# GLA mixer and conv FFN on one core: output weights' gate products and block sums by GpSimd, SiLU and decays in a fixed order, FFN token loads ahead of norms, positions set anew

## The chip, the cores and the metric

The kernel runs on 1 core of one Trainium2 chip. Its time is the device time of one execution in microseconds. A core has TensorE (PE: matmuls; PEld: their weight loads), VectorE (DVE), ScalarE (ACT), GpSimd (POOL) and SyncE (SP, which issues most transfers here), each with an instruction queue that it works off in order, and engines for transfers between DRAM and the on-chip memories (SBUF, and PSUM, where matmuls accumulate).

## The reference

One layer of a decoder trunk: a gated linear attention (GLA) mixer, then a gated MLP with a causal convolution (conv FFN), each followed by a residual and a layer norm. There are 2048 tokens of 1024 features, in float32. Cut to what matters:

```python
def gla_mixer(h, w_in, w_a2, b_a, norm_g, w_o):        # 4 heads, dk 128, dv 256, chunks of 64 tokens
    q, k, v, r, a_lr = split(h @ w_in)
    log_a = log_sigmoid(a_lr @ w_a2 + b_a) / 16        # the decays
    bcum = cumsum(log_a, within a chunk)
    q_dec, k_inv, k_dec = q * exp(bcum), k * exp(-bcum), k * exp(blast - bcum)
    o = tril(q_dec @ k_inv.T) @ v + q_dec @ state      # state = state * exp(blast) + k_dec.T @ v
    o = o * rsqrt(mean(o * o) + eps) * norm_g
    return (o * silu(r)) @ w_o

def conv_ffn(h, w_up, conv_w, conv_b, w_down):
    u, g = split(h @ w_up)                             # 2 x 2816
    return (silu(causal_conv3(u) + conv_b) * g) @ w_down

def post_norm_residual(x, cs, w_mod, b_mod, ln_gain, ln_bias, sublayer):
    shift, scale, gate = split(cs @ w_mod + b_mod)     # cs = silu(c)
    y = sublayer(x * (1 + scale) + shift)
    return layer_norm(alpha * x + (1 + gate) * y, ln_gain, ln_bias)
```

The factor (1 + gate) of the mixer belongs to columns of w_o, so it can be multiplied into w_o before that product.

## The kernel before

**Products.** A float32 matrix is split into a high part (a cast on ScalarE, L104) and a low part (a subtraction on VectorE, L107), and each product of two tiles is three matmuls: high by high, high by low, low by high (mm3, L110 to L112). Large products are done in two-by-two blocks with seven block products in place of eight, in the order 0, 1, 5, 4, 6, 3, 2; the block sums that this needs of weights and tokens are done by `add` (L352), and accumulated results leave PSUM by `keep` (L446 to L448: a copy on ScalarE with a raised priority, names p and u). The bank that is copied is accumulated further by the next product, so that product waits for the copy.

**Stages, with their time in the trace.** Until about 60 us: modulated tokens, Q and K of the first block. Then, in units of TensorE's time that the tables of the program count: v_group(0) (units 0 to 14), r_group(0) (14 to 34, 4 iterations of r_iter), v_group(1) (34 to 48), r_group(1) (48 to 88, 8 iterations, about 320 to 497 us). An r_iter makes one 256-column block of the gate r or of q and k for two token blocks by seven products; with `prev` it finishes the iteration before: r_gate, r_up and r_end drain the banks, apply SiLU to r in halves and store it. From unit 88 (B0) follow the three segments of the last projections (SEG: Q of the second half, and the two output products OO0 and OO1) with the 16 (token block, head) pairs of the attention among them (head_l, head_r, ... head_n, head_d), the first layer norm (load_z, ln1, ln1_kt), until about 850; then the FFN up (to 1660) and down (to 2107).

**Decays.** For each of 16 (token block tb, head h) `decays` (L595 on) takes a tile A3 loaded from DRAM by a3_load (L590 to L592, two units earlier), makes one matmul (L607), and on ScalarE bias (L611), Abs (L612), Exp (L615), Ln (L620), on VectorE a minimum and a scan (L621, L622), then two Exp (L624, L625), and stores them (e_d, L626 and L627). SiLU and Exp/Ln are in different function tables of ScalarE; between them stands an ACT_TABLE_LOAD. `order(later, earlier)` pins an order of two instructions; last_silu and last_exp remember the last of each kind.

**Output weights.** w_fold(q, n) (L1105) loads one of 8 tiles of w_o (128x1024, name wo), multiplies it by 1 + gate (G, L1112) and stores it (wf_d); w_mix(q, n) (L1116) makes four block sums of each four tiles (L352) and stores them (wfc_d). The output products read both later. The gate's last piece is L297 (388 us).

**What sets the order.** `at_unit(u, f)` puts a step at a unit of TensorE's time; that gives the step's place and priority, and a scheduler then orders every engine's instructions by priorities and an estimate of when operands are ready. `tc.high_priority(offset)` raises a place. Only in the part from unit 88 is TensorE's order written out by hand. The tables (H_AT, STEP, XP_AT, D_AT, W..._AT, LN_AT, F_AT and so on) hold the units. All loads and stores are issued by SyncE (`load` and `store`), in order; a store that waits for its data holds up what stands behind it.

**FFN start.** first_w, part_end, x_first(0), x_first(1), first_w1, first_w2 (placed by F_AT) load the first weight tiles and token blocks of the FFN and make their block sums and splits; ln1 of the third token block (LN_AT[2]) falls in the same time, as do the last evictions of the output product (z).

Of the kernel before, what the change touches and what calls it, by code (L numbers as in the profile page):

```python
# [38 lines left out]
def kernel(  # L39
# [405 lines left out]
    def keep(po, name):  # L445
        t = t2p.tile([P, 512], F32, tag="t2", name=name)  # L446
        with tc.high_priority(offset=600):
            return t, nc.scalar.copy(t, po)  # L448
# [5 lines left out]
    if True:  # L454
# [9 lines left out]
        made = set()  # L464
        xrow = x.rearrange("(t p) d -> t p d", p=P)
# [123 lines left out]
        def a3_load(tb):  # L589
            assert ("a", tb) in made  # L590
            a3[tb] = t2p.tile([P, TB], F32R, tag="t2", name="A3")[0:96]
            load(a3[tb].bitcast(F32), a3_d[tb])  # L592

        def decays(tb, heads):
# [9 lines left out]
            A3 = a3.pop(tb)  # L604
            for h in heads:
# [20 lines left out]
                store(e_d[tb][h][:, lo], E1)  # L626
                store(e_d[tb][h][:, hi], E2)  # L627
# [80 lines left out]
        def qk_out(tb, h, pq, pk):  # L708
# [239 lines left out]
        def r_up(p, after=None):  # L948
# [4 lines left out]
            if p["W"]["kind"]:  # L953
                nc.scalar.copy(p["r0"][:, 512:1024], p["pa"])
                store(qk_d[tb][h], p["r0"])
# [5 lines left out]
            else:  # L961
                a = nc.scalar.activation(p["r0"][:, 512:1024], p["pa"], AF.Silu)
                nc.scalar.activation(p["r0"][:, 0:512], p["r0"][:, 0:512], AF.Silu)
                order(a, after)
            if last_exp:
                order(a, last_exp[-1])
            store(r_d[tb][h], p["r0"])

        def r_end(p, after=None):
# [9 lines left out]
            store(r_d[tb + 1][h], p["r1"])  # L979
# [124 lines left out]

        def w_fold(q, n):  # L1105
# [6 lines left out]
            nc.vector.tensor_tensor(rv, rv, g[:, None, :].to_broadcast([P, 2, 512]), op=ALU.mult)  # L1112
# [27 lines left out]
        R_AT = ((9.75, 10.25, 12.25), (42.75, 45.0, 45.25))  # L1140
# [3 lines left out]
        WAW_AT = (12.25, 45.75, 53.75)  # L1144
# [15 lines left out]
        M_AT = (36, 36.5, 37.75, 37.75, 40, 41, 41.75, 43.25, 51, 52, 53, 54, 55, 56, 57, 58)  # L1160
        MF_AT = (50.0, 49.5, 57.5, 62.5)
# [12 lines left out]
        WF_AT = ((69, 69.0, 70.0, 70.75), (72, 74.25, 75.5, 76.75))  # L1174
        WM_AT = ((72.0, 74.0), (82.75, 83.75))
# [5 lines left out]
        E_AT = (83.25, 85.45, 87.7, 88.45)  # L1181
# [114 lines left out]
        def head_t(H):  # L1296
# [4 lines left out]
            with tc.high_priority(offset=150):  # L1301
                nc.scalar.copy(H["KT"], pt)

        def head_a(H, g):
# [7 lines left out]
            with tc.high_priority(offset=1200):  # L1312
# [29 lines left out]
        def head_c(H, g):  # L1342
# [16 lines left out]
            with tc.high_priority(offset=600):  # L1359
# [11 lines left out]
        def head_d(H, e):  # L1371
# [4 lines left out]
            with tc.high_priority(offset=600):  # L1376
# [29 lines left out]
        def ln1_kt(tb, zs, kt, by_act=False):  # L1406
# [32 lines left out]
        def q_segment(tb):  # L1439
            key = "Q", tb  # L1440
            for ps_ in range(2):
                banks = [psum("mm", 4) for _ in range(4)]
                outs = [raw_tile("qk") for _ in range(2)]
                for u in range(4):

                    def done(n):
                        if u == 3:
# [137 lines left out]
        H_AT = (0.25, 1.5, 2.75, 4, 5, 6, 7, 8.25, 9.5, 12.75, 13.5, 14.75, 16.75, 18.5, 20, 21.5)  # L1585
        STEP = (-0.4, 0, 0.5, 0.6, 0.75, 0.2, 0.5, 0.85, 1, 1.5, 1.5, 1.6, 1.6, 2.3, 2.5)
        STEPB = (-0.5, 0, 0.5, 0.75, 1, 0.0, 0.25, 0.75, 1.0, 0.5, 1.75, 2, 2, 2.75, 3)
        for m in range(16):
            H = heads[m]
            u = B0 + H_AT[m]  # L1590
            for k, (f, *a) in zip(STEP if m < 8 else STEPB, ((head_l,), (head_s,), (head_t,), (head_a, 0), (head_a, 1), (head_v,), (head_i,), (head_b, 0),
# [3 lines left out]
                if f is head_r and m in (2, 14):  # L1595
                    k = 1.75
# [466 lines left out]
```

## Time and profile before

| what | value |
|---|---|
| runs | 2111.23, 2107.44, 2112.12 us (median 2111.23) |
| the profiled execution's own time | 2109.05 us |
| its span | 2107.0 us, granted clock 0.996 |
| TensorE busy | 2074.5 us (98%) |
| VectorE, ScalarE, GpSimd busy | 1532.0 (73%), 997.2 (47%), 109.8 us (5%) |
| SyncE's transfers | 568.16 MB, 76.6% of 16 engines' span |

A line of a group reads: line, engine, operation, output tile <- input tiles, shapes, count, then busy time in us, mean ns of one, and the idle time of the engine ahead of it with what ended it. A line of waits reads: what waited <- for what, us in total, times, longest. A line of the timeline reads: start, duration, engine, line, operation, and in brackets the idle time before it and its releaser. A line of windows gives the busy us and count of instructions of PE, PEld, DVE, ACT and POOL, then granted clock, DMA share and GB/s. A line of transfers has the median time from issue to landing at its end.

### The profile page before, as it was taken

To read this page: it belongs to the slowest core of one execution; us is meant where nothing else is said; L and a number is where in the kernel's file an instruction comes from. 1 tells how busy PE (TensorE), PEld (TensorE's weight loads), DVE (VectorE), ACT (ScalarE), POOL (GpSimd) and SP (SyncE) were. 2 spreads that over 40 slices of the span, in tenths; PEclk is the share of its full clock that TensorE was granted. 3 is DMA by queue.
4 is the path that set the end of the run, shared out by engine and by line. 5 is a ranking of instruction groups with operands and counts; after the bars stand their busy time and mean duration, and the time that the engine had idled before them with its cause. 6 is when DMAs were issued, how large, how long until landed. Compare 5 with 4: busy or idle time off the path is not lost.

```text
span 2107.0 us, 26146 instructions
## 1 busy us (share of the span) xinstructions
PE 2074.5 (98%) x9333; PEld 1713.0 (81%) x9333; DVE 1532.0 (73%) x2028; ACT 997.2 (47%) x1401; POOL 109.8 (5%) x254
## 2 busy tenths in 40 slices
PE   9999999999999999999999999999999999999998
PEld 7887887778888887888888888888888888888886
DVE  6855757776697868967787887666666797577557
ACT  4649735674554534644444453333333443354332
POOL 0000000001121301100000000000000000030001
PEclk9999999999999999999999999999999999999999
DMA  9787888689878897866796679777787897677662
GB/s 335 306 294 267 277 298 288 248 298 326 325 291 294 313 355 285 304 234 212 280 322 215 221 263 330 275 267 262 255 277 260 278 340 236 205 253 246 194 199 88
DMA packets 196210, 569.82 MB, mean 270 GB/s; under 512 B 25392, under 2 KB 36016, under 8 KB 186864
## 3 DMA queue, kind: packets, MB, share of 16 engines
q1 hardware_dynamic: 196080, 568.16, 76.6%
q8 instruction: 73, 1.20, 0.2%
q14 instruction: 57, 0.47, 0.1%
HBM read 366.49 MB, written 201.59 MB: 270 GB/s over the span
## 4 chain that ended last, share of the span: by engine, by line
PE 82%; DVE 6%; DMA 5%; ACT 4%; issue 2%; POOL 0%; SPq 0%; DVEq 0%; ACTq 0%; POOLq 0%
PE ps_mm L110 17%; PE ps_mm L112 17%; PE ps_mm L111 17%; PE ps_w L112 8%; PE ps_w L111 8%; PE ps_w L110 8%; PE ps_w L1354 1%; PE ps_w L1326 1%; PE ps_w L1356 1%; PE ps_w L1310 1%; DMA A<-a_d 1%; DMA mraw<-in_mws_dram 1%; PE ps_w L1412 1%; DVE hl L107 1%; PE ps_w L1375 1%
## 5 line engine op out<-in xcount | busy, mean ns | idle before, releaser
L110 PE MATMUL ps_mm<-xc,hl 128*128 128x512 f32 x920 | 362.6, 394 | 9.4 <-ACT u L448 7.7
L111 PE MATMUL ps_mm<-xc,hl 128*128 128x512 f32 x920 | 359.6, 391 | 0.0
L112 PE MATMUL ps_mm<-xc,hl 128*128 128x512 f32 x920 | 358.2, 391 | 0.0
L110 PEld LDWEIGHTS ps_mm<-xc,hl 128*128 128x128 f32 x920 | 173.5, 189 | 50.6 <-ACT u L448 10.9
L112 PEld LDWEIGHTS ps_mm<-xc,hl 128*128 128x128 f32 x920 | 173.6, 189 | 36.6 <-DVE hl L107 0.2
L111 PEld LDWEIGHTS ps_mm<-xc,hl 128*128 128x128 f32 x920 | 173.5, 189 | 35.9 <-issue 0.5
L112 PE MATMUL ps_w<-xc,hl 128*128 128x512 f32 x464 | 180.6, 389 | 2.0 <-DVE hl L107 2.0
L110 PE MATMUL ps_w<-xc,hl 128*128 128x512 f32 x464 | 180.8, 390 | 0.1
L111 PE MATMUL ps_w<-xc,hl 128*128 128x512 f32 x464 | 180.5, 389 | 0.0
L1660 DVE SCALAR_TENSOR_TENSOR ct<-U,cw_sb,ct 128x512 f32<-128x512 f32 x176 | 131.7, 748 | 23.8 <-ACT ct L1654 21.3
L104 ACT CAST hl<-wu 128x1024 fp32r<-128x1024 f32 x90 | 94.7, 1052 | 100.2 <-PE ps_mm L112 73.0
L448 ACT COPY u<-ps_mm 128x512 f32<-128x512 f32 x112 | 65.3, 583 | 161.9 <-PE ps_mm L112 153.4
L104 ACT CAST dhl<-raw 128x1024 fp32r<-128x1024 f32 x57 | 60.0, 1053 | 155.2 <-PE ps_mm L112 96.5
L107 DVE TENSOR_TENSOR hl<-wu,hl 128x1024 fp32r<-128x1024 f32 x90 | 109.9, 1221 | 28.0 <-ACT hl L104 27.5
L107 DVE TENSOR_TENSOR dhl<-raw,dhl 128x1024 fp32r<-128x1024 f32 x57 | 69.5, 1220 | 64.1 <-ACT dhl L104 64.0
L104 ACT CAST hl<-raw 128x1024 fp32r<-128x1024 f32 (+1 forms) x63 | 59.9, 954 | 106.7 <-PE ps_mm L112 42.0
L107 DVE TENSOR_TENSOR hl<-raw,hl 128x1024 fp32r<-128x1024 f32 (+1 forms) x63 | 69.1, 1102 | 53.0 <-ACT hl L104 52.9
L112 PEld LDWEIGHTS ps_w<-xc,hl 128*128 128x128 f32 x464 | 87.1, 188 | 20.5 <-DVE hl L107 2.4
L104 ACT CAST hl<-wg 128x1024 fp32r<-128x1024 f32 x56 | 58.9, 1052 | 94.6 <-PE ps_mm L112 85.5
L111 PE MATMUL ps_mm<-dhl 128*128 128x512 f32 x264 | 102.7, 389 | 0.0
L112 PE MATMUL ps_mm<-dhl 128*128 128x512 f32 x264 | 102.7, 389 | 0.0
L110 PE MATMUL ps_mm<-dhl 128*128 128x512 f32 x264 | 102.7, 389 | 0.0
(286 smaller groups left out, 4726.5 us busy)
## 6 DMA issues: line engine op xcount, KB each, us to landing
hc_d<-ct SPq DMA_DIRECT2D x154, 256.0 KB, 3.0
raw<-hc_d SPq DMA_DIRECT2D x70, 512.0 KB, 4.3
draw<-wc_d SPq DMA_DIRECT2D x70, 512.0 KB, 4.7
wu<-in_wup_dram SPq DMA_DIRECT2D x44, 512.0 KB, 5.1
wg<-in_wup_dram SPq DMA_DIRECT2D x44, 512.0 KB, 4.5
wh_d<-hl SPq DMA_DIRECT2D x22, 1024.0 KB, 4.8
hl<-wh_d SPq DMA_DIRECT2D x22, 1024.0 KB, 6.2
mraw<-in_mws_dram SPq DMA_DIRECT2D x40, 512.0 KB, 5.8
```

What stands on the lines that cost most here:

```text
L104: accs["copy"] = nc.scalar.copy(h, src)
L107: return nc.vector.tensor_tensor(l, src if lsrc is None else lsrc, h.bitcast(F32), op=ALU.subtract)
L110: nc.tensor.matmul(po, a[0], b[0], start=first, stop=False, skip_group_check=resumed)
L111: nc.tensor.matmul(po, a[0], b[1], start=False, stop=False, skip_group_check=resumed)
L112: return nc.tensor.matmul(po, a[1], b[0], start=False, stop=last, skip_group_check=resumed)
L448: return t, nc.scalar.copy(t, po)
L1310: nc.tensor.matmul(pav[:, i], KI[:, s * P:s * P + P], Q[:, s], start=True, stop=True)
L1326: nc.tensor.matmul(pst[:, s % 2 * DV:s % 2 * DV + DV], KTt[:, s * P:s * P + P], v[s], start=True, stop=True)
L1354: nc.tensor.matmul(pos_, at[:, i], v[s], start=True, stop=st is None)
L1356: nc.tensor.matmul(pos_, Q[:, s, 0:128], st, start=False, stop=True)
L1375: nc.tensor.transpose(pt[:, s * P:s * P + P], on[:, s, e * P:e * P + P], ident)
L1660: nc.vector.scalar_tensor_tensor(ct, U[:, o + i:o + i + 512], cw_sb[:, j, i:i + 1], ct, op0=ALU.mult, op1=ALU.add)
```

## The change

- c and the modulation biases (c_sb, mbs_sb) are loaded from ScalarE's queue at the start, in place of SyncE's.
- `keep` has a priority offset of 1200 in place of 600. In the attention part the offsets of four operations change: the K transposes' copy 150 to 60, the attention masks 1200 to 300, the copy of o 600 to 0, the gating of o 600 to 1200; that of the first head's loads goes from 1200 to 60.
- r_up: the second half's SiLU is pinned behind the last exponentials and the first half's behind it; r_up's SiLU now counts as the last one (last_silu), so that later decays' exponentials are pinned behind it.
- a3_load's tile is kept per (token block, heads), not per token block. There are 16 loads as before.
- The products of w_fold and the sums of w_mix are GpSimd's (W_ENG).
- Nearly all tables of units change, a little each. st_e to st_m are names for `store` (ACT_ST is empty), and D_BY is 1: these change nothing.

On ScalarE, the rows between two copies u of r_group(0), in the stretch 183 to 193 us of the profile; r, mn and az are tiles of the gate and of decays. Before:

```order
L104 CAST hl<-wu 128x1024
L624 ACT_TABLE_LOAD
L624 ACTIVATE mn<-az 128x512
L611 ACTIVATE mn<-ps_w,ba_sb 128x512
L625 ACTIVATE az<-az 128x512
L962 ACT_TABLE_LOAD
L962 ACTIVATE r_1526<-ps_mm 128x512
L612 ACTIVATE az<-mn 128x512
L104 CAST h_1832<-s_1672 128x512
L615 ACT_TABLE_LOAD
L615 ACTIVATE az<-az 128x512
L448 COPY u_1826<-ps_mm 128x512
```

The same stretch of the change (from here on its lines are 2 to 10 further):

```order
L448 COPY u_1734<-ps_mm 128x512
L626 ACTIVATE mn<-az 128x512
L104 CAST hl<-wu 128x1024
L627 ACTIVATE az<-az 128x512
L964 ACT_TABLE_LOAD
L964 ACTIVATE r_1554<-ps_mm 128x512
L968 ACTIVATE r_1554<-r_1554 128x512
L448 COPY u_1812<-ps_mm 128x512
```

Two of three table loads left the stretch, the next decays' first operations stand behind the copy, and both halves of the SiLU share one load. Over the program the order has 34 ACT_TABLE_LOAD rows before and 25 now.

On SyncE, at the first four tiles of w_o in r_group(1), about 399 to 417 us. wf_d are the folded tiles, wfc_d their sums, A the decays' loads (A_3439 and A_3457 are for the ninth and tenth decays, in this order). Before:

```order
L1113 DMA wf_d_252<-wo 128x1024
L967 DMA r_d_2_342<-r_3164 128x1024
L1113 DMA wf_d_254<-wo 128x1024
L979 DMA r_d_2_346<-r_3242 128x1024
L592 DMA A_3439<-a_d_266 96x512
L940 DMA wu<-in_wab_dram 128x1024
L1125 DMA wfc_d_0_258<-wo 128x1024
L941 DMA wg<-in_wab_dram 128x1024
L1125 DMA wfc_d_0_262<-wo 128x1024
```

The change:

```order
L1122 DMA wf_d_250<-wo 128x1024
L594 DMA A_3382<-a_d_266 96x512
L974 DMA r_d_2_342<-r_3161 128x1024
L943 DMA wg<-in_wab_dram 128x1024
L1122 DMA wf_d_252<-wo 128x1024
L1122 DMA wf_d_254<-wo 128x1024
L986 DMA r_d_2_346<-r_3258 128x1024
L942 DMA wu<-in_wab_dram 128x1024
L1134 DMA wfc_d_0_258<-wo 128x1024
L1134 DMA wfc_d_0_262<-wo 128x1024
L943 DMA wg<-in_wab_dram 128x1024
L594 DMA A_3457<-a_d_266 96x512
```

The tenth decays' load (A_3457) now stands behind the stores of two sums, which wait for GpSimd; the ninth's stands behind two folded tiles. GpSimd's own order has the 16 operations as four folds, four sums, four folds, four sums, ahead of the attention's small operations.

On VectorE, at the FFN start (about 825 to 840 us; z are evictions of the output product, xs and xc the FFN's token block, hl<-wg and hl<-wu splits of its first weights). Before:

```order
L352 TENSOR_TENSOR z<-z,ps_mm 128x512 x3
L107 TENSOR_TENSOR hl<-wu,hl 128x1024
L352 TENSOR_TENSOR xs<-xs 128x1024
L352 TENSOR_TENSOR z<-z,ps_mm 128x512
L352 TENSOR_TENSOR xs<-xs,xc 128x1024
L107 TENSOR_TENSOR hl<-wg,hl 128x1024
L352 TENSOR_TENSOR xs<-xs 128x1024
L107 TENSOR_TENSOR xc<-xc 128x1024
L352 TENSOR_TENSOR xs<-xc,xs 128x1024
L107 TENSOR_TENSOR xc<-xs,xc 128x1024
L107 TENSOR_TENSOR xc<-xc 128x1024
L107 TENSOR_TENSOR xc<-xs,xc 128x1024
```

The change:

```order
L352 TENSOR_TENSOR xs<-xs,xc 128x1024
L352 TENSOR_TENSOR z<-z,ps_mm 128x512
L352 TENSOR_TENSOR xs<-xs 128x1024
L107 TENSOR_TENSOR xc<-xc 128x1024
L352 TENSOR_TENSOR xs<-xc,xs 128x1024
L107 TENSOR_TENSOR xc<-xs,xc 128x1024
L107 TENSOR_TENSOR xc<-xc 128x1024
L107 TENSOR_TENSOR xc<-xs,xc 128x1024
L352 TENSOR_TENSOR z<-z,ps_mm 128x512
L107 TENSOR_TENSOR hl<-wg,hl 128x1024
```

Six operations of the token block moved ahead of hl<-wg. TensorE's order moved with them: of the product with hl<-wg, the first matmul with the low part stood at row 3164 of TensorE's order and stands now at row 3187.

The diff, cut to its core (of the tables, the rows that the text speaks of):

```diff
-    load(c_sb, cT)
+    nc.scalar.dma_start(c_sb, cT)
...
-    load(mbs_sb, mbs)
+    nc.scalar.dma_start(mbs_sb, mbs)
...
     def keep(po, name):
         t = t2p.tile([P, 512], F32, tag="t2", name=name)
-        with tc.high_priority(offset=600):
+        with tc.high_priority(offset=1200):
             return t, nc.scalar.copy(t, po)
...
         def at_decays(u, tb, heads):
-            at_unit(u - 2, a3_load, tb)
+            at_unit(u - 2, a3_load, tb, heads)
...
-        def a3_load(tb):
+        def a3_load(tb, heads):
             assert ("a", tb) in made
-            a3[tb] = t2p.tile([P, TB], F32R, tag="t2", name="A3")[0:96]
-            load(a3[tb].bitcast(F32), a3_d[tb])
+            a3[tb, heads] = t2p.tile([P, TB], F32R, tag="t2", name="A3")[0:96]
+            load(a3[tb, heads].bitcast(F32), a3_d[tb])
...
             else:
                 a = nc.scalar.activation(p["r0"][:, 512:1024], p["pa"], AF.Silu)
-                nc.scalar.activation(p["r0"][:, 0:512], p["r0"][:, 0:512], AF.Silu)
                 order(a, after)
+                if last_exp:
+                    order(a, last_exp[-1])
+                a2 = nc.scalar.activation(p["r0"][:, 0:512], p["r0"][:, 0:512], AF.Silu)
+                order(a2, a)
+                a = a2
             if last_exp:
                 order(a, last_exp[-1])
-            store(r_d[tb][h], p["r0"])
+            last_silu.append(a)
+            st_r(r_d[tb][h], p["r0"])
...
+        W_ENG = (nc.vector, nc.gpsimd)[1]
...
-            nc.vector.tensor_tensor(rv, rv, g[:, None, :].to_broadcast([P, 2, 512]), op=ALU.mult)
+            W_ENG.tensor_tensor(rv, rv, g[:, None, :].to_broadcast([P, 2, 512]), op=ALU.mult)
...
-                add(nc.vector, r22, r21, r22)
-                add(nc.vector, r21, r11, r21, SUB)
+                add(W_ENG, r22, r21, r22)
+                add(W_ENG, r21, r11, r21, SUB)
                 return
-            add(nc.vector, r11, r22, r11, SUB)
-            add(nc.vector, r12, r12, r11, SUB)
+            add(W_ENG, r11, r22, r11, SUB)
+            add(W_ENG, r12, r12, r11, SUB)
...
-        D_AT = (17, 20, 22.75, 26.75, 50.5, 54, 58, 62, 70, 72, 74, 76, 78, 80, 82, 84)
+        D_AT = (17, 20, 23.0, 26.75, 50.5, 54, 58, 60, 68, 70, 72, 76, 78, 80, 82, 84)
...
-        XP_AT = (16.5, 19.75)
+        XP_AT = (14.5, 21.75)
...
-        WF_AT = ((69, 69.0, 70.0, 70.75), (72, 74.25, 75.5, 76.75))
-        WM_AT = ((72.0, 74.0), (82.75, 83.75))
+        WF_AT = ((69, 69.0, 70.5, 71.25), (73.75, 75.5, 76.25, 77.5))
+        WM_AT = ((72.0, 74.5), (84.25, 84.5))
...
-            with tc.high_priority(offset=600):
+            with tc.high_priority(offset=0):
                 nc.scalar.copy(on[:, 2 * g:2 * g + 2].rearrange("p s c -> p (s c)"), po)
...
-            with tc.high_priority(offset=600):
+            with tc.high_priority(offset=1200):
                 nc.vector.scalar_tensor_tensor(sr[:, e], pt, ng_sb[:, e:e + 1], sr[:, e], op0=ALU.mult, op1=ALU.mult)
...
-        H_AT = (0.25, 1.5, 2.75, 4, 5, 6, 7, 8.25, 9.5, 12.75, 13.5, 14.75, 16.75, 18.5, 20, 21.5)
+        H_AT = (0.75, 1.5, 2.75, 4, 5, 6, 7, 8.25, 9.5, 12.75, 13.5, 14.75, 16.75, 18.5, 20, 21.5)
...
-        LN_AT = ((17, 18.25, 17.5, 18.0), (21, 21.25, 21.5, 21.75), (32.5, 32.75, 33, 33.25))
+        LN_AT = ((17, 18.25, 17.5, 18.0), (21, 21.25, 21.5, 21.75), (34.25, 34.5, 34.75, 35))
...
-        F_AT = (28, 29.5, 34, 32, 34.5)
+        F_AT = (28, 29.5, 32.5, 32, 34)
```

More of the change, by code (lines that the diff above doesn't have):

```diff
@@ L464 @@
         made = set()
+        ACT_ST = ''
+        st_e, st_q, st_x, st_r, st_n, st_m = [nc.scalar.dma_start if c in ACT_ST else nc.gpsimd.dma_start if c.upper() in ACT_ST else store for c in "eqxrnm"]
         xrow = x.rearrange("(t p) d -> t p d", p=P)
@@ L603, in decays @@
             assert ("a", tb) in made
-            A3 = a3.pop(tb)
+            A3 = a3.pop((tb, heads))
             for h in heads:
@@ L625, in decays @@
                 last_exp.append(nc.scalar.activation(E2, az, AF.Exp, scale=-1.0 / 16.0))
-                store(e_d[tb][h][:, lo], E1)
-                store(e_d[tb][h][:, hi], E2)
+                st_e(e_d[tb][h][:, lo], E1)
+                st_e(e_d[tb][h][:, hi], E2)
                 made.add(("E", tb, h))
@@ L644, in keep_a @@
             nc.scalar.copy(t, pa[0:96])
-            store(ak_d[hf], t)
+            st_e(ak_d[hf], t)
             made.add(("ak", hf))
@@ L978, in r_end @@
             last_silu.append(a)
-            store(r_d[tb + 1][h], p["r1"])
+            st_r(r_d[tb + 1][h], p["r1"])
         staged = []
@@ L1143 @@
                 at_unit(V0 + u, f, *a)
-        WAW_AT = (12.25, 45.75, 53.75)
+        WAW_AT = (12.75, 45.75, 53.75)
         for u in WAW_AT:
@@ L1148 @@
         at_unit(GR_AT[0], gate_rows, 1, X)
-        D_AT = (17, 20, 22.75, 26.75, 50.5, 54, 58, 62, 70, 72, 74, 76, 78, 80, 82, 84)
-        for m, u in enumerate(D_AT):
-            at_decays(u, m // 4, (m % 4,))
-        XP_AT = (16.5, 19.75)
+        D_AT = (17, 20, 23.0, 26.75, 50.5, 54, 58, 60, 68, 70, 72, 76, 78, 80, 82, 84)
+        D_BY = 1
+        for m in range(0, 16, D_BY):
+            at_decays(D_AT[m], m // 4, tuple(range(m % 4, m % 4 + D_BY)))
+        XP_AT = (14.5, 21.75)
         for pr in range(2):
@@ L1237, in open_act @@
             pools["act"] = actx.enter_context(tc.tile_pool(name="actp", bufs=1, reuse_waits="tile"))
-            with tc.high_priority(offset=1200):
+            with tc.high_priority(offset=60):
                 head_l(heads[0])
@@ L1300, in head_t @@
             H["KT"] = t2p.tile([P, TB], F32, tag="t2", name="KTt")
-            with tc.high_priority(offset=150):
+            with tc.high_priority(offset=60):
                 nc.scalar.copy(H["KT"], pt)
@@ L1311, in head_a @@
             am = attm[H["h"] % 2 * 2 + g]
-            with tc.high_priority(offset=1200):
+            with tc.high_priority(offset=300):
                 nc.vector.copy_predicated(am[0:64], mask[0:64, None, :].to_broadcast([64, 2, P]), pav[0:64, :, 0:128])
@@ L1396, in ln1 @@
             normalise(zs[t], after)
-            store(zn_d[tb * 4 + t], zs[t])
+            st_n(zn_d[tb * 4 + t], zs[t])
         cols = {}
@@ L1595 @@
                 if f is head_r and m in (2, 14):
-                    k = 1.75
+                    k = -1.25
                 at_unit(u + k, f, H, *a)
         SEG = (("Q", 1), ("OO", 0), ("OO", 1))
-        XO_AT = (7, 8.75, 10.75, 12.75, 14.75, 15.5, 18.0)
+        XO_AT = (7, 8.75, 10.75, 12.75, 14.5, 13.5, 18.0)
         for u, i in zip(XO_AT, OP):
             at_unit(B0 + u, o_x, i)
-        YX_AT = (19.75, 21.75)
-        YS_AT = (23.0, 23.0)
+        YX_AT = (19.5, 22.5)
+        YS_AT = (24.5, 24.5)
         for n in range(2):
```

34 lines of the change are left out of this document (17 added, 17 removed).

## The prediction

> **What bounds the kernel now.** I read the page first, then what TensorE waited for, then the stretches where it lost time.
>
> ```profile
> span 2107.0 us, 26146 instructions
> PE 2074.5 (98%) x9333; PEld 1713.0 (81%) x9333; DVE 1532.0 (73%) x2028; ACT 997.2 (47%) x1401; POOL 109.8 (5%) x254
> PE ps_mm L110 <- ACT u L448: 10.2, 9, 3.2
> PE ps_w L1375 <- ACT on L1369: 2.3, 3, 1.0
> PE ps_w L112 <- DVE hl L107: 2.0, 1, 2.0
> PE ps_w L607 <- DMA A<-a_d: 1.9, 2, 1.5
> PE ps_mm L112 <- DVE xg L107: 1.5, 1, 1.5
> ```
>
> TensorE is idle for 2107.0 − 2074.5 = 32.5 us, and the change touches no product. So all it can win is a part of those 32.5 us, plus the slow matmuls that follow a stall. The longest wait is for ScalarE's copy of a PSUM bank (u, by keep), which frees the bank for the next product. The stretches show where the other engines are short (PE, PEld, DVE, ACT, POOL busy, then clock, DMA):
>
> ```profile
> 175.00:200.00 25.00, 23.21 (x94) 18.46 (x93) 15.52 (x20) 24.66 (x30) 0.00 (x0) 0.93 0.77 268
> 200.00:225.00 25.00, 25.00 (x111) 20.68 (x111) 15.46 (x17) 24.45 (x31) 0.00 (x0) 1.00 0.58 199
> 425.00:450.00 25.00, 24.39 (x105) 19.24 (x104) 20.22 (x23) 19.85 (x30) 0.00 (x0) 1.00 0.88 311
> 825.00:850.00 25.00, 21.67 (x89) 16.08 (x88) 23.55 (x27) 16.11 (x21) 0.20 (x2) 1.00 0.69 243
> 1000.00:1025.00 25.00, 25.00 (x120) 20.85 (x120) 18.31 (x26) 11.00 (x17) 0.38 (x3) 1.00 0.77 263
> ```
>
> ScalarE is full in 175–225 (24.66 and 24.45 of 25), VectorE in 825–850 (23.55). Later the FFN runs without a gap (1000–1025), so it has nothing to give.
>
> **SiLU and decays in a fixed order.** A table load stands before each change of function on ScalarE:
>
> ```profile
> L597 ACT ACT_TABLE_LOAD x7 | 9.0, 1283 | 0.1
> L624 ACT ACTIVATE mn<-az 128x512 f32<-128x512 f32 x16 | 10.1, 632 | 7.2 <-DVE az L622 7.0
> 183.57 0.57 ACT L448 COPY u<-ps_mm 128x512 f32<-128x512 f32 x1
> 184.04 1.05 ACT L104 CAST hl<-wu 128x1024 fp32r<-128x1024 f32 x1
> 185.11 1.28 ACT L624 ACT_TABLE_LOAD   x1
> 191.08 1.28 ACT L615 ACT_TABLE_LOAD   x1
> 192.91 0.57 ACT L448 COPY u<-ps_mm 128x512 f32<-128x512 f32 x1
> 193.53 0.58 PE L110 MATMUL ps_mm<-xc,hl 128*128 128x512 f32 x1 [1.79 <-ACT u L448]
> 197.28 0.40 PE L110 MATMUL ps_mm<-xc,hl 128*128 128x512 f32 x1
> ```
>
> The rows on order count 34 loads before and 25 after, so 9 × 1.283 = 11.5 us of ScalarE go. At 183–193 the work between two copies was 192.91 − 184.04 = 8.9 us with three loads. In the changed order it is one load (1.28), one weight cast (1.05), two exponentials and two half SiLUs at 0.63: 4.8 us. The second copy could then run at 184.0 + 4.8 = 188.8, and TensorE arrives at 193.53 − 1.79 = 191.7. The new order adds no wait between engines: the SiLUs stand behind the copy and the exponentials of their own engine, and behind them a copy (after one product more) and casts that had 1.28 us loads there before. The wait goes. So do the slow matmuls: nine took 197.28 − 193.53 = 3.75 us, where the rate of 200–225 (111 in 25.00, 0.225 each) asks for 2.0. Together **−3.5 us**; I see no case that makes it less than −1.8.
>
> The longest stall and the next decays:
>
> ```profile
> 169.89 0.80 PE L110 MATMUL ps_mm<-xc,hl 128*128 128x512 f32 x1 [3.16 <-ACT u L448]
> 343.17 0.47 PE L607 MATMUL ps_w<-A,w2s 96*128 96x512 f32 x1 [1.51 <-DMA A<-a_d]
> ```
>
> Up to 165 us ScalarE's and SyncE's orders are the same in both kernels but for one SiLU, whatever XP_AT says; ScalarE is held there by the token prepared through DRAM (x_prep). 169.89 stays: 0. The remaining 10.2 − 3.2 − 1.8 = 5.2 us of waits for u are spread over seven places of both r_groups. Fewer table loads, and a copy with more priority (keep, 600 to 1200), work there: **−2** (bounds 0 and −5). At 343.17 the load of A was queued behind two stores of decays and now stands ahead of them: **−1.5** (0 to −1.9).
>
> **Gate products and sums on GpSimd.** Sixteen operations leave VectorE:
>
> ```profile
> L352 DVE TENSOR_TENSOR wo<-wo 128x1024 f32<-128x1024 f32 x8 | 9.8, 1219 | 1.1 <-DMA wf_d<-wo 1.0
> L1112 DVE TENSOR_TENSOR wo<-wo,G 128x1024 f32<-128x1024 f32 x8 | 9.7, 1221 | 4.0 <-DMA wo<-in_wab_dram 4.0
> L1253 POOL MEMSET attm<- 128x256 f32 x4 | 1.1, 312 | 0.0
> L190 POOL MEMSET maskf<- 128x128 f32 x1 | 0.2, 204 | 0.0
> ```
>
> That frees 19.5 us of VectorE, which in 425–450, its fullest stretch there, has 4.8 of 25 us free anyway: worth nothing on the path by itself. GpSimd's price isn't in the trace. Its memsets grow by 108 ns for 128 columns, so 1024 columns of one stream cost at least 0.2 + 0.84 × 0.9 = 1.0 us, and three streams (two read, one written) 2.7. I take t = 2.3, nearer the upper end, since two operands share what one memset has alone. The Trainium skill (GPSIMD Engine Reference, Elementwise) gives 4497 ns for 2048 columns, an estimate of 2.25 here; the sum would be the same by it.
>
> What is late next is on SyncE's queue, which is in order: the stores of these tiles wait for GpSimd, and loads of A stand behind them. The rows:
>
> ```profile
> 388.35 0.68 DVE L297 SCALAR_TENSOR_TENSOR G<-ps_w,graw 128x512 f32<-128x512 f32 x1
> wf_d<-wo SPq DMA_DIRECT2D x8, 512.0 KB, 3.4
> A<-a_d SPq DMA_DIRECT2D x8, 192.0 KB, 4.1
> 414.57 0.40 PE L607 MATMUL ps_w<-A,w2s 96*128 96x512 f32 x1
> ```
>
> On the old clock, the gate is ready at 389.0, and the first fold begins about 389.5. Four folds end at 389.5 + 4t. The sums overwrite tiles that are being stored, so they wait for the landing (3.4, say 5 with the queue). Two sums, 2t, release the two stores ahead of the load for the tenth decays, whose issue and landing take 0.4 + 4.1. Counted in the orders, the ninth decays' product was the 1582nd matmul of 512 columns and ran at 414.57; now the tenth's is the 1583rd, so TensorE needs this load at 414.8 on that clock. The stall is 389.5 + 6t + 9.5 − 414.8 = 6t − 15.8: nothing at t = 2.3, 0.4 at 2.7, 5 at 3.5. The loads ahead and behind have more room. I put **+2** for this and for VectorE's share (bounds 0 and +10).
>
> **Attention.** Heads, output loads and the three priorities move, mostly by exchanging neighbours on VectorE; the distance from the norm (L1369) to its transposes (L1375) stays, so its 2.3 us stay. The 1.5 us for xg may go, since xg now stands between evictions instead of behind seven: **−1** (bounds −5 and +3: all waits of this part, or as many new ones as xg and the norm cost now).
>
> **FFN start.**
>
> ```profile
> 832.55 0.50 PE L112 MATMUL ps_w<-xc,hl 128*128 128x512 f32 x1 [2.00 <-DVE hl L107]
> 823.11 0.69 DVE L352 TENSOR_TENSOR z<-z,ps_mm 128x512 f32<-128x512 f32 x1 [0.64 <-PE ps_mm L112]
> 827.26 1.23 DVE L107 TENSOR_TENSOR hl<-wu,hl 128x1024 fp32r<-128x1024 f32 x1 [0.74 <-ACT hl L104]
> 828.40 1.22 DVE L352 TENSOR_TENSOR xs<-xs 128x1024 f32<-128x1024 f32 x1
> 831.27 1.22 DVE L107 TENSOR_TENSOR hl<-wg,hl 128x1024 fp32r<-128x1024 f32 x1
> 844.02 1.21 DVE L107 TENSOR_TENSOR hl<-wu,hl 128x1024 fp32r<-128x1024 f32 x1
> ```
>
> Before, VectorE idled 0.64 to 0.74 four times at evictions and a split (823–827), 2.7 us in all, and did most of the token block behind hl<-wg. In the new order six operations of that block, 1.14 apart (827.26 to 828.40), come ahead of hl<-wg and fill that idle time: this split ends near 832.4 + 6.8 − 2.7 = 836.5. But TensorE's order moved too and asks for its low half 23 matmuls later: 832.55 − 2.00 + 23 × 0.225 = 835.7. The next split (844.02) comes some 3.5 us earlier, with those six done. I count 1 us of stall where 825–850 lost 25.00 − 21.67 = 3.3, and a little won just around it: **−3** (bounds −4.5 and +2, if the later hl<-wg is waited for after all).
>
> c and its table from ScalarE's queue move only the first 3 us: 0 (±1).
>
> **Sum.** −3.5 − 2 − 1.5 + 2 − 1 − 3 = −9 us. The profiled execution took 2109.05, the three runs 2107.44 to 2112.12 with a median of 2111.23; the four average 2110. That gives **2101 us**. A measurement here tells 0.2% (4.2 us) from no change.
>
> **Rivals.**
>
> *No change, 2108.* Only 193.53 is won and the waits for u move to the next thing late, as at 169.89: 2110 − 3.5 + 2 = 2108.5. For it: seven of the nine waits for u are short (5.2 us in all) and stand among casts which stay. Against: three different stretches improve in the order.
>
> *Slower, 2117.* GpSimd and VectorE exclude each other, and the tenth decays' load comes late. The trace shows that GpSimd can be held:
>
> ```profile
> 1038.95 1.22 DVE L107 TENSOR_TENSOR hl<-wu,hl 128x1024 fp32r<-128x1024 f32 x1
> 1039.07 1.15 POOL L1731 COPY halo<-U 128x2 f32<-128x2 f32 x1 [16.19 <-DVE U L352]
> L1731 POOL COPY halo<-U x22: 184/185/2245, 866.3 to 1274.6; 128x2 f32<-128x2 f32 x22
> ```
>
> A copy of 185 ns took 1.15 us and ended with the split beside it. One such wait per operation gives t = 2.3 + 1.2 = 3.5, a stall of 5. Without GpSimd's term the sum is −11; so 6t − 15.8 = 11, t = 4.5, is the point from which nothing is left, and t = 5.5 gives 2110 − 11 + 17 = 2116, and 2117 with a little for VectorE, held in return. It needs two to three waits in each operation, so VectorE would have to cut into one that is running; against it stands that VectorE is idle 19% of its fullest stretch there.
>
> *Held in turn, 2107.* Each operation of GpSimd waits once for VectorE and then holds it to its own end. From the rows above, that is t = 3.5 and a stall of 5, and VectorE is held for up to 16 × 2.3 = 37 us where 19.5 were freed, 17 more in a stretch of about 80 us with some 20 us idle; I put 3 us for splits that come late by it: 2110 − 11 + 5 + 3 = 2107. For it: the copy that ended with the split. Against: VectorE's own durations stay at 1.22 beside GpSimd in that row, though for a copy too short to show it. This is what the Trainium skill says (SBUF — State Buffer, the shared port pair): whichever of GpSimd and a VectorE operation with two SBUF inputs starts first has the port to its end.
>
> *More, 2093.* The attention's and all of u's waits shrink too, or 169.89 goes with its slow matmuls (5 us): 2110 − 9 − 8. Little speaks for the latter, as ScalarE's order there is unchanged.
>
> **How the numbers follow.** Forecast 0.51, more 0.12, no change 0.11, held in turn 0.12, slower 0.14. Held in turn lies at the edge of 0.2%: a sixth of it counts as faster. Faster: 0.51 + 0.12 + 0.02 = 0.65; same 0.11 + 0.10 = 0.21; slower 0.14. The range 2090 to 2113 takes the gain to −20 on the one side; on the other it takes in the no-change case and a stall up to t = 4.9, and leaves out the worst of the slower one. The forecast's own range is 2096 to 2106.
>
> **What would show it.** Right: 25 table loads, no wait at 193, 169.89 still there, no wait for A near 343, folds of 2–3 us on GpSimd, and at 825–850 more than 23 us of TensorE. Wrong: folds over 4 us, a wait of L607's successor for A around 400–415 of several us, or new waits for attention's tiles after 500.

## The result and the profile after

The changed kernel takes 2121.08 us (median of six runs, 2118.03 to 2130.59). The kernel before takes 2112.16 us (2107.44 to 2113.91, six runs). The ratio is 1.0053, with a 95% interval of 1.0037 to 1.0070: slower by about 11 us. The forecast was 2101, and its range ended at 2113. The profiled execution took 2120.55 us with a span of 2118.8, so the two profiles that are compared below differ by 2118.8 − 2107.0 = +11.8 in their spans.

The head of the page and the waits of TensorE in the changed kernel:

```profile
span 2118.8 us, 26149 instructions
PE 2077.1 (98%) x9333; PEld 1715.0 (81%) x9333; DVE 1536.9 (73%) x2012; ACT 984.7 (46%) x1392; POOL 155.2 (7%) x270
PE ps_w L609 <- DMA A<-a_d: 8.9, 2, 4.6
PE ps_mm L110 <- ACT u L448: 7.5, 6, 4.3
PE ps_w L112 <- DVE hl L107: 5.9, 1, 5.9
```

The copies u cost less than before (7.5 against 10.2), and ScalarE is busy 12.5 us less (984.7 against 997.2), as its nine table loads fewer should make it. But two loads of A and one split of VectorE now cost 14.8 us, where waits of those two kinds cost 3.9. VectorE is the line to stop at: it has 16 operations fewer, worth 19.5 us, and is busy 4.9 us *more*. The stretches from 375 to 475 (PE, PEld, DVE, ACT, POOL, clock, DMA). Before, the first two of them:

```profile
375.00:400.00 25.00, 24.14 (x106) 18.93 (x105) 18.00 (x26) 19.46 (x25) 0.00 (x0) 1.00 0.61 218
400.00:425.00 25.00, 24.65 (x109) 20.05 (x109) 19.42 (x22) 15.67 (x21) 0.00 (x0) 1.00 0.87 318
```

The change, all four:

```profile
375.00:400.00 25.00, 18.29 (x77) 14.23 (x78) 17.58 (x18) 17.43 (x23) 11.57 (x4) 0.94 0.48 167
400.00:425.00 25.00, 20.64 (x83) 16.56 (x82) 18.21 (x13) 10.16 (x14) 10.61 (x4) 0.91 0.62 211
425.00:450.00 25.00, 25.00 (x104) 20.16 (x105) 11.57 (x15) 22.29 (x32) 9.73 (x4) 0.94 0.82 317
450.00:475.00 25.00, 20.01 (x79) 15.80 (x78) 21.13 (x18) 13.73 (x22) 11.07 (x4) 0.87 0.67 239
```

TensorE did 343 matmuls in these 100 us. GpSimd has four operations in each stretch. VectorE did 18 operations in 17.58 us and 13 in 18.21 us, where it had done 26 in 18.00 and 22 in 19.42 before: it is as busy with far fewer. In the third stretch, though, TensorE waits for nothing beside GpSimd's four operations: it is busy for all of the 25.00 us. The timeline of VectorE and GpSimd in the first stretch shows why:

```profile
384.51 11.57 POOL L1121 TENSOR_TENSOR wo<-wo,G 128x1024 f32<-128x1024 f32 x4 [382.78 <-DVE G L297]
385.48 2.84 DVE L624 TENSOR_TENSOR_SCAN az<-smask,mn 128x512 f32<-128x512 f32 x1
388.82 0.68 DVE L352 TENSOR_TENSOR r<-ps_mm,p 128x512 f32<-128x512 f32 x1
389.53 1.54 DVE L352 TENSOR_TENSOR s<-wu,wg 128x512 f32<-128x512 f32 x1
391.11 2.76 DVE L352 TENSOR_TENSOR wg<-wg 128x512 f32<-128x512 f32 x1
393.91 2.71 DVE L352 TENSOR_TENSOR wu<-wg,wu 128x512 f32<-128x512 f32 x1
396.54 0.68 DVE L107 TENSOR_TENSOR h<-s,h 128x512 fp32r<-128x512 f32 x1
397.75 1.21 DVE L107 TENSOR_TENSOR hl<-wg,hl 128x1024 fp32r<-128x1024 f32 x1
399.01 0.80 PE L112 MATMUL ps_w<-xc,hl 128*128 128x512 f32 x1 [5.86 <-DVE hl L107]
```

The four folds run from 384.51 to 396.08. In that time wg and wu, operations of 128x512 with both operands in SBUF, take 2.76 and 2.71 us, about the length of a fold (2.39 undisturbed), and after 396.08 the same kind takes 0.68. The scan at 385.48, also with both operands in SBUF, takes 2.84 where it takes 1.22 undisturbed; s, which comes in the last third of a fold, takes 1.54. The one with an operand in PSUM (r<-ps_mm,p at 388.82) takes 0.68 in the middle of it. So block sums and splits queue up behind GpSimd, TensorE waits 5.86 us for the split hl, and then runs 11 matmuls in 4.87 us (399.01 to 403.88, where 2.5 would do).

### The profile page after: what moved, and what is told of

Its sections match the earlier page's. It is cut to its first block, busy times and chain, and to the rows that moved or that the text cites. A ratio compares the mean times of both kernels' runs of the same rounds, so it can differ in the third digit from the quotient of the medians.

```text
span 2118.8 us, 26149 instructions
## 1 busy us (share of the span) xinstructions
PE 2077.1 (98%) x9333; PEld 1715.0 (81%) x9333; DVE 1536.9 (73%) x2012; ACT 984.7 (46%) x1392; POOL 155.2 (7%) x270
## 4 chain that ended last, share of the span: by engine, by line
PE 82%; DMA 7%; DVE 5%; ACT 3%; issue 2%; POOL 1%; SPq 0%; DVEq 0%; ACTq 0%; POOLq 0%
PE ps_mm L110 17%; PE ps_mm L112 17%; PE ps_mm L111 17%; PE ps_w L112 8%; PE ps_w L110 8%; PE ps_w L111 8%; PE ps_w L1336 1%; PE ps_w L1364 1%; DMA mraw<-in_mws_dram 1%; PE ps_w L1366 1%; PE ps_w L1320 1%; DMA graw<-in_mwg_dram 1%; DVE hl L107 1%; PE ps_w L1422 1%; DVE xc L107 0%
## 5 line engine op out<-in xcount | busy, mean ns | idle before, releaser
L112 PE MATMUL ps_w<-xc,hl 128*128 128x512 f32 x464 | 182.9, 394 | 5.9 <-DVE hl L107 5.9
L110 PE MATMUL ps_w<-xc,hl 128*128 128x512 f32 x464 | 182.6, 394 | 0.0
L111 PE MATMUL ps_w<-xc,hl 128*128 128x512 f32 x464 | 182.5, 393 | 0.0
L112 PEld LDWEIGHTS ps_w<-xc,hl 128*128 128x128 f32 x464 | 88.3, 190 | 25.1 <-DVE hl L107 6.5
L110 PEld LDWEIGHTS ps_w<-xc,hl 128*128 128x128 f32 x464 | 88.5, 191 | 18.7 <-ACT hl L104 0.4
L111 PEld LDWEIGHTS ps_w<-xc,hl 128*128 128x128 f32 x464 | 88.3, 190 | 18.6
L111 PE MATMUL ps_mm<-dhl 128*128 128x512 f32 x264 | 102.7, 389 | 0.0
L112 PE MATMUL ps_mm<-dhl 128*128 128x512 f32 x264 | 102.7, 389 | 0.0
```

Source lines behind the costliest of these rows:

```text
L110: nc.tensor.matmul(po, a[0], b[0], start=first, stop=False, skip_group_check=resumed)
L111: nc.tensor.matmul(po, a[0], b[1], start=False, stop=False, skip_group_check=resumed)
L112: return nc.tensor.matmul(po, a[1], b[0], start=False, stop=last, skip_group_check=resumed)
```

## The experiments

Theory after the result: a wide operation of GpSimd and an operation of VectorE that reads two operands in SBUF exclude each other, and the waits at 399, 425 and 471 come from it. Rivals: the new positions cost the time; or SyncE's queue does, where loads of A stand behind stores that wait for GpSimd (what the prediction feared).

**GpSimd's part taken back (vec), and GpSimd's part alone (gps_only).**

```diff
-        W_ENG = (nc.vector, nc.gpsimd)[1]        # vec, on the change
+        W_ENG = (nc.vector, nc.gpsimd)[0]
...
-            nc.vector.tensor_tensor(rv, rv, ...)  # gps_only, on the kernel before; the four sums of w_mix alike
+            nc.gpsimd.tensor_tensor(rv, rv, ...)
```

> The change with its 16 operations on wo put back on VectorE, all else kept. Theory (GpSimd and VectorE hold each other, and the stores that wait for GpSimd hold the loads of A): the waits at 399 (5.9 us), 425 (4.4) and 471 (4.6) go with their slow matmuls, no VectorE operation of 128x512 takes 2.7 us any more, and what is left is the sum of the other terms: 2098 to 2104, below the kernel before. Rival (the new positions and priorities cost the time, GpSimd only shows it): 2112 to 2120, with the waits at 425 and 471 for A still there. In both the waits for the norm at 647 and 702 (3.3 us in all) stay.

> The kernel before with only the 16 operations on wo given to GpSimd, old positions. Theory: VectorE's operations with two SBUF inputs stretch from 0.69 to about 2.7 us beside them and the loads of A come late: 2120 to 2135, slower than before by 10 us or more. Rival (positions cost the time): 2108 to 2116, no change.

The kernel before was run again beside the experiments, with medians of 2108.3 to 2109.2 us, and the ratios of the experiments are to these runs. vec takes 2102.35 us, a ratio of 0.9968 to the kernel before (0.9954 to 0.9983). gps_only takes 2134.1 us, 1.0113 (1.0089 to 1.0137). So GpSimd's part costs 18 us within the change (1.0053 − 0.9968 = 0.85%) and 24 us in the kernel before, and the rest of the change gains 6.7 us. The rival of the positions falls: they make up for part of GpSimd's cost. vec is faster than both kernels. Its page and its stretches:

```profile
span 2098.8 us, 26120 instructions
PE 2072.8 (99%) x9333; PEld 1713.3 (82%) x9333; DVE 1531.2 (73%) x2028; ACT 985.9 (47%) x1392; POOL 112.6 (5%) x254
375.00:400.00 25.00, 23.88 (x105) 18.57 (x104) 17.39 (x24) 19.25 (x26) 0.00 (x0) 1.00 0.64 225
400.00:425.00 25.00, 24.46 (x107) 19.69 (x106) 18.46 (x22) 18.70 (x26) 0.00 (x0) 1.00 0.79 285
425.00:450.00 25.00, 24.14 (x105) 19.19 (x104) 17.88 (x21) 19.25 (x29) 0.00 (x0) 1.00 0.85 307
450.00:475.00 25.00, 24.87 (x108) 19.80 (x107) 19.86 (x22) 19.87 (x33) 0.00 (x0) 1.00 0.88 307
```

425 matmuls in these 100 us against 343: 82 fewer at about 0.23 us are 19 us, and the spans differ by 20.0: nearly all of the loss stands in this stretch. And VectorE's 2012 operations of the change took 1536.9 − (1531.2 − 19.5) = 25 us longer than the same operations here. The same subtraction gives 4 us for gp_memset below, where nothing is held, so it is a little high: the twelve VectorE operations that are stretched in the change's timeline lose 23 us in all. Even so GpSimd held back more of VectorE than the 19.5 us that it took over. The third group, the folds from 427 to 444, stretched none.

**SyncE's queue or held VectorE? (a_act).**

```diff
-            load(a3[tb, heads].bitcast(F32), a3_d[tb])
+            nc.scalar.dma_start(a3[tb, heads].bitcast(F32), a3_d[tb])
```

> The change with the 16 loads of A issued from ScalarE's queue in place of SyncE's. It tells the two costs of GpSimd's part apart: loads of A held behind stores that wait for GpSimd, and VectorE held by GpSimd itself. If both count: the waits for A at 425 and 471 (8.9 us, and some 4 us of slow matmuls behind them) go, the wait for VectorE's hl at 399 (5.9 us) stays: 2107 to 2114. If only the held VectorE counts, and the loads of A were late for what it did to ScalarE and the weight buffers: 2117 to 2124. If the loads of A were all of it: 2098 to 2104.

It takes 2141.85 us, 1.0156 (1.0137 to 1.0174): outside all three, slower even than the change. The waits for A did not go: there are six of 14.2 us in all, the longest 7.4, where the change has two of 8.9. The edit has a cost of its own, since ScalarE works its queue off in order: at 422.32 ScalarE has been idle for 5.08 us behind a load of A that waits for its buffer. So the time doesn't tell the two costs apart, but the chain of waits does for the wait near 425, since the load of A leaves from another queue and still at the same event. First of the change, then of this kernel (start, us, what):

```profile
416.86 3.42 DVE hl L107
420.29 0.61 DVE r L352
420.91 3.81 DMA A<-a_d
424.76 0.79 PE ps_w L609
```

```profile
417.91 3.41 DVE hl L107
421.33 0.61 DVE r L352
421.96 6.77 DMA A<-a_d
428.78 0.81 PE ps_w L609
```

In both, the load starts 0.01 to 0.02 us after VectorE's add r ends. That add frees the buffer that the load fills (p, u and A share buffers), and it stands behind a split that GpSimd held for 3.4 us in place of 1.22. The stores ahead of it had left by then, as SyncE's timeline of the change shows:

```profile
410.78 3.14 SPq L1134 DMA_DIRECT2D wfc_d<-wo  x2
420.31 0.33 SPq L943 DMA_DIRECT2D wg<-in_wab_dram  x1
420.91 0.32 SPq L594 DMA_DIRECT2D A<-a_d  x1
```

They are issued by 413.9; the weight load between waits for the buffer that the same split reads. So the load of A was late by the held VectorE, not by the stores. The wait at 471 has the same origin by another way. There the load stands on SyncE's queue behind a weight load (L128), which leaves when a held split has ended; the stores of the second tiles' sums come only after it:

```profile
463.25 3.36 DVE hl L107
466.63 0.38 SPq L128
467.12 3.91 DMA A<-a_d
```

What the stores alone would cost, with VectorE not held, no run here shows. Why the transfer near 422 took 6.8 us in a_act instead of 3.8 was not followed up.

**One group of operations (gp_sums).** The folds go back to VectorE, the sums stay GpSimd's.

```diff
-            W_ENG.tensor_tensor(rv, rv, g[:, None, :].to_broadcast([P, 2, 512]), op=ALU.mult)
+            nc.vector.tensor_tensor(rv, rv, g[:, None, :].to_broadcast([P, 2, 512]), op=ALU.mult)
```

> The change with the eight folds back on VectorE and the eight sums still GpSimd's. If the held VectorE is the whole cost, each group of four operations costs the wait that stands beside it: the one near 399 (5.9 us and 2 of slow matmuls) goes with the folds, the two for A near 425 and 471 (8.9 and some 4) stay with the sums, since the load of A waits for a buffer that VectorE's next add frees: 2108 to 2115. If the stores behind the folds on SyncE's queue were what made the loads of A late, these go too: 2100 to 2106.

2115.97 us, 1.0029 (1.0016 to 1.0042): against vec's 0.9968 that is 13 of GpSimd's 18 us, from half of its operations, and a little over what was expected. The profiled execution took 2110.42 us, the least of the ten, so its waits are rather too small. The wait near 399 is gone with the folds. Beside the sums stand three, but not the two for A that were expected: A has 1.7 us at 459, and ScalarE's name is on the two largest:

```profile
417.33 0.80 PE L110 MATMUL ps_mm<-xc,h 128*128 128x512 f32 x1 [3.75 <-ACT u L448]
466.66 0.79 PE L110 MATMUL ps_mm<-xc,h 128*128 128x512 f32 x1 [4.35 <-ACT u L448]
409.35 2.87 DVE L623 SCALAR_TENSOR_TENSOR mn<-mn,az 128x512 f32<-128x512 f32 x1
412.14 2.86 DVE L352 TENSOR_TENSOR wu<-wg,wu 128x512 f32<-128x512 f32 x1
416.17 0.63 ACT L626 ACTIVATE mn<-az 128x512 f32<-128x512 f32 x1 [8.48 <-DVE az L624]
416.71 0.57 ACT L448 COPY u<-ps_mm 128x512 f32<-128x512 f32 x1
```

ScalarE itself is idle for 8.48 us. The copy u stands behind an exponential on its queue, that behind VectorE's scan, and the scan behind two operations that GpSimd held for 2.9 us each. So the same hold reaches TensorE as a late split (399), a late buffer for A (425) or a late copy (417), by what stands next in order.

**How long one holds the other (gp_quarter).** Each operation is cut into four of 128x256.

```diff
-            W_ENG.tensor_tensor(rv, rv, g[:, None, :].to_broadcast([P, 2, 512]), op=ALU.mult)
+            for q4 in range(4):
+                c4 = slice(q4 % 2 * 256, q4 % 2 * 256 + 256)
+                W_ENG.tensor_tensor(rv[:, q4 // 2, c4], rv[:, q4 // 2, c4], g[:, c4], op=ALU.mult)
...
-                add(W_ENG, r22, r21, r22)          # and the other three sums
+                [add(W_ENG, r22[:, c:c + 256], r21[:, c:c + 256], r22[:, c:c + 256]) for c in range(0, 1024, 256)]
```

> The change with each of GpSimd's 16 operations cut into four of 128x256. If GpSimd holds VectorE for one instruction at a time: GpSimd's pieces take about 0.7 us alone, VectorE's operations of 128x512 between them 1.3 us in place of 2.7, each piece waits up to one VectorE operation, so a fold takes 4 to 6 us from first to last piece; the wait at 399 shrinks to 0 to 3 us, and the loads of A come later still: 2118 to 2135. If the two share bandwidth and nothing is held: VectorE's operations stay as long beside GpSimd as before, a fold stays at 2.4 to 3.3 us, and the time stays: 2118 to 2124.

2120.3 us, 1.0047 (1.0028 to 1.0065): the same as the change, and inside what both theories allowed, so the durations decide. VectorE in the first folds, and GpSimd's pieces (min/median/max ns):

```profile
393.65 1.12 DVE L352 TENSOR_TENSOR wg<-wg 128x512 f32<-128x512 f32 x1
394.81 1.11 DVE L352 TENSOR_TENSOR wu<-wg,wu 128x512 f32<-128x512 f32 x1
L352 POOL TENSOR_TENSOR wo<-wo x32: 721/1178/1770, 410.1 to 472.2; 128x256 f32<-128x256 f32 x32
```

2.7 us became 1.1 with a quarter of the length of GpSimd's instructions, and GpSimd's pieces stretch from 0.72 to 1.77: the two alternate, an instruction of one, an instruction of the other. Sharing of bandwidth would not depend on how GpSimd's work is cut. The wait near 399 fell from 5.9 to 2.3 us, but the last load of A came still later (4.9 us), and the median stayed. (The profiled execution took 2127.89 us, the longest of the four; a wait of 4.1 us at 709, which the change has as 1.4, is in it too.)

**What in GpSimd's operation holds (gp_copy, gp_memset).** The products and sums are left out; the sixteen operations only copy a tile of 128x1024, or only set one.

```diff
-            W_ENG.tensor_tensor(rv, rv, g[:, None, :].to_broadcast([P, 2, 512]), op=ALU.mult)
+            W_ENG.tensor_copy(r, r)                # gp_memset: W_ENG.memset(r, 0.5)
...
-                add(W_ENG, r22, r21, r22)          # and the other three sums
+                W_ENG.tensor_copy(r22, r21)        # gp_memset: W_ENG.memset(r22, 0.5)
```

> The change with GpSimd's 16 products and sums replaced by 16 copies of one tile of 128x1024 (one operand read in SBUF; the gate's product and the sums are left out, so the output is another). If GpSimd holds VectorE by two reads only, VectorE's operations of 128x512 stay at 0.69 us beside the copies and the time is that without GpSimd's operations: 2098 to 2106. If one read is enough, they stretch to the length of a copy (1.0 to 1.5 us by the memset rows): VectorE loses at most 16 x 1.5 = 24 us where it gave up 19.5, 2102 to 2112.

> The change with GpSimd's 16 products and sums replaced by 16 memsets of 128x1024 (nothing read; products and sums are left out, so the output is another). If it is GpSimd's reading that holds VectorE, its operations beside a memset stay at 0.69 and 1.22 us: 2098 to 2105. If any wide operation of GpSimd holds it, they stretch to the memset's 1.0 us and more: 2100 to 2110, with operations of 128x512 at 1.0 us or over beside a memset.

gp_copy: 2107.1 us, 0.9990 (0.9976 to 1.0004), inside the range for one read being enough. gp_memset: 2104.01 us, 0.9977 (0.9967 to 0.9987), which is vec's gain within the intervals and inside both of its ranges, so the durations decide. The first two lines are copies and one VectorE operation beside them, the others memsets and what stands beside them:

```profile
423.85 1.52 DVE L623 SCALAR_TENSOR_TENSOR mn<-mn,az 128x512 f32<-128x512 f32 x1
426.34 1.85 POOL L1131 COPY wo<-wo 128x1024 f32<-128x1024 f32 x1
```

```profile
414.84 1.22 DVE L624 TENSOR_TENSOR_SCAN az<-smask,mn 128x512 f32<-128x512 f32 x1
415.51 0.96 POOL L1132 MEMSET wo<- 128x1024 f32 x1 [2.24 <-DMA wf_d<-wo]
415.98 0.67 DVE L352 TENSOR_TENSOR wu<-wu 128x512 f32<-128x512 f32 x1
L1121 POOL MEMSET wo<- x8: 952/954/959, 334.9 to 412.3; 128x1024 f32 x8
```

A copy takes 1.04 us undisturbed and up to 1.85 beside VectorE, and VectorE's 0.69 becomes 1.52 beside a copy: one read is enough. A memset takes 0.95 to 0.97 in all sixteen cases, and VectorE keeps its 0.67 and 1.22 beside it: without a read nothing is held. This is the rule of the Trainium skill (SBUF — State Buffer, the shared port pair), and these rows agree with it in each part that they can show: two SBUF inputs on one side, a read on the other, and the whole instruction. The copies and memsets do not wait for the gate, so they stand elsewhere in time than the folds; the durations are comparable, the waits of TensorE are not.

**The other terms (silu_only, ffn_only, vec_nosilu, vec_m).** silu_only is the kernel before with r_up's order of the change; ffn_only is the kernel before with F_AT, LN_AT and LT_AT of the change; vec_nosilu is vec with the old r_up; vec_m is vec with the old M_AT.

```diff
-                nc.scalar.activation(p["r0"][:, 0:512], p["r0"][:, 0:512], AF.Silu)   # silu_only; vec_nosilu is the reverse
                 order(a, after)
+                if last_exp:
+                    order(a, last_exp[-1])
+                a2 = nc.scalar.activation(p["r0"][:, 0:512], p["r0"][:, 0:512], AF.Silu)
+                order(a2, a)
+                a = a2
...
+            last_silu.append(a)
...
-        F_AT = (28, 29.5, 34, 32, 34.5)           # ffn_only, with LN_AT and LT_AT
+        F_AT = (28, 29.5, 32.5, 32, 34)
...
-        M_AT = (36.5, 36.5, 37.75, 37.75, 40, 41, 41.75, 44.25, 52, 53, 53, 54.25, 54.5, 56, 57, 59)   # vec_m
+        M_AT = (36, 36.5, 37.75, 37.75, 40, 41, 41.75, 43.25, 51, 52, 53, 54, 55, 56, 57, 58)
```

> The kernel before with only r_up's SiLUs pinned behind the last exponentials. By the prediction's first term 25 table loads, the wait at 193 and its slow matmuls go (-3.5 us), and some of the other waits for u (0 to -2): 2105 to 2109. Rival (ScalarE's copies are held by other work): 2110 to 2113, the wait at 193 or one near it is still there.

> The kernel before with only the FFN start's tables (F_AT, LN_AT, LT_AT) of the change. By the prediction's last term TensorE loses 3 us less between 825 and 865: 2107 to 2110. Rival (a token block earlier only moves the wait to later splits): 2110 to 2114.

> The change with its operations on wo on VectorE and r_up's SiLUs as they were before: 38 table loads in the order in place of 25. If the fixed order carries the gain that is left without GpSimd: 2106 to 2112, with a wait for u near 193 again. Rival (positions and priorities carry it): 2099 to 2105.

> The change with its operations on wo on VectorE and the old table of the modulation steps (M_AT). There the wait at 351 for the sum of modulation products (2.0 us, with slow small matmuls behind it) is new. If that table brings it, it goes and the time is 2097 to 2102, under the same kernel with the new table; if not, 2100 to 2106.

- silu_only: 2109.01 us, 0.9999 (0.9987 to 1.0012). The wait at 193 is gone as expected, and the time is the same. Its profile has 4.50 us at 171 and 3.35 at 831, where the kernel before has 3.16 and 2.00.
- ffn_only: 2106.98 us, 0.9989 (0.9976 to 1.0002). The wait of 2.00 at 832 went; five of 0.43 to 0.73 stand around it instead, 3.1 us in all, as much as the kernel before waits there with its 2.00, a 0.74 and a 0.39. TensorE is busy for 22.92 us of 825 to 850 in place of 21.67. A gain of 2 us would fit, but it is not shown.
- vec_nosilu: 2108.11 us, 0.9998 (0.9987 to 1.0010). Without the fixed order the gain of vec is gone: there is a wait for A of 2.9 us at 204 and one for u of 3.9 at 169, where vec has 2.2, but none near 193, where it was expected. So the new positions and priorities alone bring nothing, the fixed order alone nothing, and both together 6 to 7 us. What in the positions the order needs was not taken apart.
- vec_m: 2108.24 us, 0.9994 (0.9982 to 1.0007). The wait at 351 went, with waits for A of 1.7 and 2.0 us in its place. The time is above both ranges, so the expectation was wrong, and the new table is probably worth keeping: the interval just touches vec's. The profiled execution took 2102.12 us, the least of the twelve, so the trace doesn't show what the median lost.

## Why the prediction was wrong

**The step that failed** is the term "+2 for this and for VectorE's share (bounds 0 and +10)". It measures +18 us in the change, beyond its upper bound, and +24 alone. Three things in it were wrong.

- *What is held.* The text counted 19.5 us of freed VectorE time as worth nothing on the path. gp_memset agrees with that: it frees the same time, holds nothing and is no faster than vec, though its memsets stand elsewhere in time. But the text took VectorE's loss to be small as well. One of its own rivals, "Held in turn", named what happens, with a bound on the held time that was kept (up to 37 us; about 23 measured). It got a chance of 0.12, and 3 us for splits that come late, beside 5 for a load of A, which made 2107 where 2121 was measured. VectorE's operations come in runs: from 389.5 to 396.6 s, wg and wu stand one behind the other, all with two SBUF operands, and wait for the rest of one fold and then for a whole fold each. Idle time elsewhere in the stretch doesn't help against that, and behind the run stands a split that TensorE needs. The price should have been made for the run: its holds, then the stall, then the slow matmuls, at each group that meets such a run. Three of the four did (the waits at 399, 425 and 471).
- *The evidence against it.* "VectorE's own durations stay at 1.22 beside GpSimd in that row" rested on a copy of 185 ns that started while a VectorE operation was running. That row shows GpSimd waiting; since GpSimd came second there, it can't show what VectorE loses when it comes second itself.
- *Where the loads of A hang.* The formula 6t − 15.8 followed the stores on SyncE's queue. t was nearly right: 2.3 was put, and the rows below have 2.4 undisturbed and 2.7 in the middle. By the formula the stall at 2.7 is 0.4; it was 4.4. The 5 us put for the folded tiles to land were too few: GpSimd stood idle for 12.3 us before its first sum, as the last tiles' stores left only at 401.2, behind a late store of r. Even so the two stores of sums had left by 413.9, and with 0.4 + 4.1 for the load it could have landed at 418.4, before TensorE came for it at 424.76 − 4.36 = 420.4 (itself late by the wait at 399). The load waited for a buffer that VectorE's held add frees. So the slower rival had the right place, the loads of A after 400, and the wrong way to it: its point, t = 4.5, did not decide.

```profile
L1121 POOL TENSOR_TENSOR wo<-wo,G x8: 2387/2674/3327, 384.5 to 441.5; 128x1024 f32<-128x1024 f32 x8
```

**What held.** The table loads fell from 34 to 25, and the work between two copies at 183.69 to 187.59 is 3.9 us where 4.8 were worked out:

```profile
183.69 1.05 ACT L104 CAST hl<-wu 128x1024 fp32r<-128x1024 f32 x1
185.28 1.28 ACT L964 ACT_TABLE_LOAD   x1
187.59 0.58 ACT L448 COPY u<-ps_mm 128x512 f32<-128x512 f32 x1
169.69 0.80 PE L110 MATMUL ps_mm<-xc,hl 128*128 128x512 f32 x1 [4.27 <-ACT u L448]
```

There is no wait at 193, the one at 169 is still there, none for A near 343, and none for xg near 795. At the FFN start the wait for hl<-wg went, and small ones (0.5 at 846.85, 0.4 to 0.7 at the next three) came behind it. Without GpSimd's term the sum was −11; vec measures −6.7 (−3.6 to −9.7). The terms were somewhat large, and −3.5 for the wait at 193 was not additive: alone it gives nothing.

All six signs that the prediction named for being right came true, but for one fold of 3.3 us (the others took 2.4 to 2.8). Of its signs for being wrong one did clearly, a wait of several us for A. None of the signs looked at how long VectorE's operations take beside GpSimd, which is where the time went.

## What to carry to other kernels

Before an elementwise operation with operands in SBUF is moved from VectorE to GpSimd, look at what VectorE does beside it. In these runs its operations with two SBUF operands waited for the end of the GpSimd instruction that was running, and what the move freed was given back (19.5 us freed, about 23 held). VectorE's operations with an operand in PSUM, and any beside GpSimd's memsets, which read nothing, took their usual time. Look for a run of such VectorE operations just ahead of something TensorE needs; its share of busy time says nothing about that. Where GpSimd's work met no such run (the folds from 427 to 444), TensorE waited for nothing.

## What the runs showed of the hardware that was not expected

- GpSimd's add or product of two tiles of 128x1024 takes 2.39 us undisturbed and up to 3.3 beside VectorE in the change, a copy 1.04, a memset 0.95.
- The wait near 169 differs from kernel to kernel by more than some terms of the sum: 3.16 us before, 2.45 in ffn_only, which changes only tables of steps some 600 us later, 4.27 after. A gain of 2 us read from one trace at such a place is not yet a gain; the ratios over twelve runs are what told silu_only and vec apart.
